# A rotary embedding on one core: a cast store of zeros at the head of the software queue, and batch 0 stored in one piece

## The chip, the core and the metric

The kernel runs on one core of a Trainium2 chip. The core has several engines that run side by side, each on its own instruction stream: VectorE (DVE in the profile) does elementwise arithmetic, ScalarE (ACT) copies and casts here, GpSimd (POOL) issues most of the transfers, SyncE (SP) issues a few others. The transfers themselves are done by 16 DMA engines, which are fed by two queues: a software queue (q0 in the profile, "software_dynamic"), whose transfers POOL issues, and a hardware queue (q1, "hardware_dynamic"), whose transfers SP issues. The transfers of the software queue can change the number type on the way (here float32 in memory, float16 on chip); this is called a cast load or a cast store below.

The metric is the device time of one execution in microseconds (us). Lower is better.

## The reference

`x` has 8 batches of 2048 positions, 16 heads and 64 elements a head, all float32; `cos` and `sin` have 2048 positions of 32 elements.

```python
x1 = x[..., :head_dim // 2]
x2 = x[..., head_dim // 2:]
cos = cos[None, :, None, :]
sin = sin[None, :, None, :]
out1 = x1 * cos - x2 * sin
out2 = x1 * sin + x2 * cos
return np.concatenate([out1, out2], axis=-1)
```

So 8 MiB of float32 are read and 8 MiB are written for each of the 8 batches, and each element meets two multiplications and one addition.

## The kernel before

**Layout.** A batch is one tile `xt` of 128 partitions. Each partition holds 16 consecutive positions (rows, `J = 16`), of 1024 elements each. On the chip the data is float16. There are five buffers for `xt` (`NBUF = 5`), so a load into a buffer has to wait until the store of the batch that used it five batches earlier has landed: the load of batch 5 waits for the store of batch 0, that of batch 6 for the store of batch 1, that of batch 7 for the store of batch 2.

**Loads.** Batch 0 comes in two parts. Its first two rows (`JA = 2`) come through the hardware queue as float32 into `head` (L36, the first transfer that SP issues), and ACT casts them into the tile (L84). SP then issues the loads of `sin_f` (L44) and `cos_f` (L45). The other 14 rows of batch 0 and all rows of the other batches are cast loads of the software queue, issued by POOL in `load` (L52).

**Arithmetic.** `rotate` does three VectorE instructions over rows `j0` to `j1` of a batch: `v = swapped halves * sin` (L73), `xt = xt * cos` (L79), `xt = xt + v` (L81). `sin_h` has a negative sign in its first half (ACT, L88 and L89), `cos_h` is a cast copy (ACT, L90). Batch 0 is rotated in two calls, first the 2 rows of `head`, then the other 14.

**Stores.** `store` (L60) issues one cast store for a batch on the software queue. Batch 0 is the exception: its row 0 (of 16) goes out alone as `first` (L100), 512 KB, and its rows 1 to 15 follow as a store of 7680 KB. The last batch leaves in three parts: rows 0 to 8 (L130, called `gate`), rows 9 to 13 (L132), and the last two rows, which ACT casts to float32 (L140) and SP stores through the hardware queue (L141), once `gate` has landed.

**Order.** The software queue works through its transfers in the order in which POOL issues them. A planner in the framework orders the instructions of each engine by the program's order and by when it thinks that each can start; the kernel adds a few edges by hand (`add_manual_dep` with `NoSync`, which order the two instructions on their engine and add no wait on a transfer). By hand, `first` stands behind the load of batch 3, the load of batch 4 behind `first`, and the rest of batch 0 behind `first`. In the profile POOL's order is: loads 0, 1, 2, 3; `first`; load 4; the rest of store 0; store 1; loads 5 and 6; stores 2 and 3; load 7; stores 4, 5 and 6; the two parts of batch 7.

Of the kernel before, what the change touches and what calls it, by code (L numbers as in the profile page):

```python
# [1 line left out]

# [4 lines left out]


@with_exitstack  # L10
def kernel(
    ctx: ExitStack,
    tc: tile.TileContext,
    x: bass.AP,
    cos: bass.AP,
    sin: bass.AP,
    out: bass.AP,
):
    nc = tc.nc
    f16 = mybir.dt.float16  # L20
    f32 = mybir.dt.float32

    B, S, H, D = x.shape
    Dh = D // 2
    P = nc.NUM_PARTITIONS
    J = S // P
    NBUF = 5

    const_pool = ctx.enter_context(tc.tile_pool(name="rope_const", bufs=1))
    io_pool = ctx.enter_context(tc.tile_pool(name="rope_io", bufs=NBUF))  # L30
    tmp_pool = ctx.enter_context(tc.tile_pool(name="rope_tmp", bufs=1))

    JA = 2
    head = const_pool.tile([P, JA, H, D], f32)
    x0 = x[0].rearrange("(p j) h d -> p j (h d)", j=J)
    nc.sync.dma_start(  # L36
        out=head.rearrange("p j h d -> p (j h d)"),
        in_=x0[:, 0:JA, :].rearrange("p j f -> p (j f)"),
    )
    sin_f = const_pool.tile([P, J, Dh], f32)  # L40
    cos_f = const_pool.tile([P, J, Dh], f32)
    cos_h = const_pool.tile([P, J, Dh], f16)
    sin_h = const_pool.tile([P, J, D], f16)
    nc.sync.dma_start(out=sin_f, in_=sin.rearrange("(p j) d -> p j d", j=J))  # L44
    nc.sync.dma_start(out=cos_f, in_=cos.rearrange("(p j) d -> p j d", j=J))  # L45

    loads = []

    def load(b):
        xt = io_pool.tile([P, J, H, D], f16)  # L50
        j0 = JA if b == 0 else 0
        dma = nc.gpsimd.dma_start(  # L52
            out=xt[:, j0:J, :, :].rearrange("p j h d -> p (j h d)"),
            in_=x[b].rearrange("(p j) h d -> p j (h d)", j=J)[:, j0:J, :].rearrange("p j f -> p (j f)"),
        )
        loads.append(dma)
        return xt

    def store(b, xt, j0=0):
        return nc.gpsimd.dma_start(  # L60
            out=out[b].rearrange("(p j) h d -> p j (h d)", j=J)[:, j0:J, :].rearrange("p j f -> p (j f)"),
            in_=xt[:, j0:J, :, :].rearrange("p j h d -> p (j h d)"),
        )

    def rotate(xt, j0, j1):
        v = tmp_pool.tile([P, J, H, D], f16)
        n = j1 - j0
        js = slice(j0, j1)
        shape = [P, n, H, 2, Dh]
        sin_b = sin_h[:, js, :].rearrange("p j (e d) -> p j e d", e=2).unsqueeze(2).to_broadcast(shape)  # L70
        cos_b = cos_h[:, js, :].unsqueeze(2).to_broadcast([P, n, 2 * H, Dh])
        xe = xt[:, js, :, :].rearrange("p j h (e d) -> p j h e d", e=2)
        nc.vector.tensor_mul(  # L73
            out=v[:, js, :, :].rearrange("p j h (e d) -> p j h e d", e=2),
            in0=xe[:, :, :, ::-1, :],
            in1=sin_b,
        )
        xw = xt[:, js, :, :].rearrange("p j h (e d) -> p j (h e) d", d=Dh)
        nc.vector.tensor_mul(out=xw, in0=xw, in1=cos_b)  # L79
        xa = xt[:, js, :, :].rearrange("p j h d -> p (j h d)")  # L80
        nc.vector.tensor_add(out=xa, in0=xa, in1=v[:, js, :, :].rearrange("p j h d -> p (j h d)"))  # L81

    tiles = [load(b) for b in range(NBUF - 1)]
    nc.scalar.copy(  # L84
        out=tiles[0][:, 0:JA, :, :].rearrange("p j h d -> p (j h d)"),
        in_=head.rearrange("p j h d -> p (j h d)"),
    )
    nc.scalar.copy(out=sin_h[:, :, Dh:D], in_=sin_f)  # L88
    nc.scalar.mul(out=sin_h[:, :, 0:Dh], in_=sin_f, mul=-1.0)  # L89
    nc.scalar.copy(out=cos_h, in_=cos_f)  # L90
    rotate(tiles[0], 0, JA)
    def part(b, j0, j1):
        return (
            out[b].rearrange("(p j) h d -> p j (h d)", j=J)[:, j0:j1, :].rearrange("p j f -> p (j f)"),
            tiles[b][:, j0:j1, :, :].rearrange("p j h d -> p (j h d)"),
        )

    def store_rows(b, j0, j1):
        dst, src = part(b, j0, j1)
        return nc.gpsimd.dma_start(out=dst, in_=src)  # L100

    first = store_rows(0, 0, 1)
    tc.add_manual_dep(
        first.ins,
        loads[NBUF - 2].ins.name,
        mybir.DependencyInfo(mybir.DependencyClass.NoSync, mybir.DependencyReason.DATA),
        reason="order of the ring",
    )
    tiles.append(load(NBUF - 1))
    tc.add_manual_dep(  # L110
        loads[NBUF - 1].ins,
        first.ins.name,
        mybir.DependencyInfo(mybir.DependencyClass.NoSync, mybir.DependencyReason.DATA),
        reason="order of the ring",
    )
    for b in range(B):
        rotate(tiles[b], JA if b == 0 else 0, J)
        if b < B - 1:
            st = store(b, tiles[b], 1 if b == 0 else 0)
            if b == 0:  # L120
                tc.add_manual_dep(
                    st.ins,
                    first.ins.name,
                    mybir.DependencyInfo(mybir.DependencyClass.NoSync, mybir.DependencyReason.DATA),
                    reason="order of the ring",
                )
        if b + NBUF < B:
            tiles.append(load(b + NBUF))
    dst, src = part(B - 1, 0, 9)
    gate = nc.gpsimd.dma_start(out=dst, in_=src)  # L130
    dst, src = part(B - 1, 9, J - JA)
    rest = nc.gpsimd.dma_start(out=dst, in_=src)  # L132
    tc.add_manual_dep(
        rest.ins,
        gate.ins.name,
        mybir.DependencyInfo(mybir.DependencyClass.NoSync, mybir.DependencyReason.DATA),
        reason="order of the ring",
    )
    dst, src = part(B - 1, J - JA, J)
    nc.scalar.copy(out=head.rearrange("p j h d -> p (j h d)"), in_=src)  # L140
    end = nc.sync.dma_start(out=dst, in_=head.rearrange("p j h d -> p (j h d)"))  # L141
    tc.add_manual_dep(
        end.ins,
        gate.ins.name,
        mybir.DependencyInfo(mybir.DependencyClass.Sync, mybir.DependencyReason.DATA),
        reason="the last rows go out behind this part",
    )


# [1 line left out]
_INS = ['x', 'cos', 'sin']  # L151
_OUTS = [((8, 2048, 16, 64), 'float32')]


# [23 lines left out]
```

## Time and profile before

| | |
|---|---|
| Time, median of 3 runs | 317.0 us (316.9 to 317.13) |
| Profiled execution, its own time | 317.48 us |
| Profiled execution, its span | 315.7 us |
| VectorE busy | 209.1 us (66%) |
| ScalarE busy | 6.8 us (2%) |
| GpSimd busy | 9.9 us (3%) |
| Software queue | 2592 packets, 99.09 MB, 98.1% of 16 engines |
| Hardware queue | 576 packets, 2.62 MB, 2.3% of 16 engines |
| Memory read and written | 67.63 MB and 67.11 MB, 427 GB/s over the span |

The span is what the trace covers; the run's own time lies 1.8 us above it. The megabytes of a queue are counted at the destination, so a cast load counts half of what it reads from memory. A share over 100% in a short window is a matter of counting: a packet is booked wholly where it starts. "Landing" is the moment at which a transfer's completion is signalled; a row that gives "us to landing" counts from the issue.

### The profile page before, as it was taken

Reading aid. Unit: us, or ns where it says so; the run is one execution under the profiler, and the core shown is the slowest. Engines: PE = TensorE matmul, PEld = TensorE weight load, DVE = VectorE, ACT = ScalarE, POOL = GpSimd, SP = SyncE. Lnnn points to the kernel's source line nnn. Section 1 sums busy time; section 2 is a strip of 40 time slices with the busy share of each in tenths; the row PEclk is TensorE's granted clock in tenths of the full one; section 3 lists DMA queues with packets and bytes.
Section 4 is the critical chain, followed back from the end, with each engine's and each line's share of the span. In section 5 each row is a group of like instructions: output and inputs, shape, how many; then the busy total and the mean of one; then the engine's idle time right before and its main releaser. Section 6 shows DMA issues by size and latency. Waiting matters only on the chain.

```text
span 315.7 us, 122 instructions
## 1 busy us (share of the span) xinstructions
DVE 209.1 (66%) x27; ACT 6.8 (2%) x6; POOL 9.9 (3%) x22
## 2 busy tenths in 40 slices
DVE  0010699999999999999999999994009994000000
ACT  4100000000000000000000000000000002000000
POOL 3000100000000000001000000100000001000000
DMA  9899999999999989999999999999999999999998
GB/s 277 183 262 208 199 220 245 199 199 199 266 199 199 498 374 523 399 332 241 224 199 199 390 407 399 399 531 266 199 249 482 399 399 515 415 399 399 432 434 330
DMA packets 3168, 101.71 MB, mean 322 GB/s; under 512 B 352, under 2 KB 352, under 8 KB 736
## 3 DMA queue, kind: packets, MB, share of 16 engines
q0 software_dynamic: 2592, 99.09, 98.1%
q1 hardware_dynamic: 576, 2.62, 2.3%
HBM read 67.63 MB, written 67.11 MB: 427 GB/s over the span
## 4 chain that ended last, share of the span: by engine, by line
DVE 25%; DMA 22%; issue 18%; another core or an unknown queue 17%; POOL 1%; ACT 1%; SPq 0%; POOLq 0%; DVEq 0%; ACTq 0%
DMA xt<-in_x_dram 12%; DMA cos_f<-in_cos_dram 10%; DVE xt L79 8%; DVE xt L81 8%; DVE v L73 8%; ACT head L140 1%; POOL out_dram L60 1%; POOL xt L52 0%; ACT cos_h L90 0%; SPq L44 0%; SPq L36 0%; POOLq L52 0%; POOLq L60 0%; DVEq L73 0%
## 5 line engine op out<-in xcount | busy, mean ns | idle before, releaser
L73 DVE TENSOR_TENSOR v<-xt,sin_h 128x16384 f16<-128x16384 f16 (+2 forms) x9 | 69.7, 7744 | 36.8 <-DMA xt<-in_x_dram 20.7
L79 DVE TENSOR_TENSOR xt<-xt,cos_h 128x16384 f16<-128x16384 f16 (+2 forms) x9 | 69.7, 7744 | 17.5 <-ACT cos_h L90 17.2
L81 DVE TENSOR_TENSOR xt<-xt,v 128x16384 f16<-128x16384 f16 (+2 forms) x9 | 69.7, 7744 | 0.3
L52 POOL DMA_DIRECT2D xt<-in_x_dram x8 | 4.4, 557 | 111.1 <-DMA out_dram<-xt 110.3
L140 ACT CAST head<-xt 128x2048 f32<-128x2048 f16 x1 | 1.9, 1897 | 229.5 <-DVE xt L81 229.5
L60 POOL DMA_DIRECT2D out_dram<-xt x7 | 3.7, 535 | 63.9 <-DVE xt L81 63.9
L130 POOL DMA_DIRECT2D out_dram<-xt x1 | 0.5, 531 | 46.3 <-DVE xt L81 46.3
L84 ACT CAST xt<-head 128x2048 f16<-128x2048 f32 x1 | 1.9, 1897 | 3.6 <-DMA head<-in_x_dram 3.6
L100 POOL DMA_DIRECT2D out_dram<-xt x1 | 0.5, 541 | 33.5 <-DVE xt L81 33.5
L84 ACT ACT_TABLE_LOAD x1 | 1.3, 1283 | 0.7 <-PEq L162 0.7
L90 ACT CAST cos_h<-cos_f 128x512 f16<-128x512 f32 x1 | 0.6, 618 | 17.8 <-DMA cos_f<-in_cos_dram 17.8
L88 ACT CAST sin_h<-sin_f 128x512 f16<-128x512 f32 x1 | 0.6, 617 | 7.2 <-DMA sin_f<-in_sin_dram 7.2
L89 ACT ACTIVATE sin_h<-sin_f 128x512 f16<-128x512 f32 x1 | 0.6, 624 | 0.0
L132 POOL DMA_DIRECT2D out_dram<-xt x1 | 0.5, 531 | 0.0
L162 POOL MEMSET const-float32-0.0<- 128x1 f32 x1 | 0.1, 99 | 0.2 <-issue 0.2
L162 POOL MEMSET const-bfloat16-1.0<- 128x1 bf16 x1 | 0.1, 102 | 0.0
L162 POOL MEMSET const-float32-1.0<- 128x1 f32 x1 | 0.1, 99 | 0.0
L162 POOL MEMSET const-uint8-127<- 128x1 uint8 x1 | 0.1, 99 | 0.0
## 6 DMA issues: line engine op xcount, KB each, us to landing
xt<-in_x_dram POOLq DMA_DIRECT2D x7, 4096.0 KB, 41.3
out_dram<-xt POOLq DMA_DIRECT2D x1, 7680.0 KB, 61.6
out_dram<-xt POOLq DMA_DIRECT2D x1, 4608.0 KB, 42.4
xt<-in_x_dram POOLq DMA_DIRECT2D x1, 3584.0 KB, 22.3
out_dram<-xt POOLq DMA_DIRECT2D x1, 2560.0 KB, 47.9
head<-in_x_dram SPq DMA_DIRECT2D x1, 1024.0 KB, 4.8
out_dram<-head SPq DMA_DIRECT2D x1, 1024.0 KB, 8.4
out_dram<-xt POOLq DMA_DIRECT2D x1, 512.0 KB, 47.1
```

The costliest lines, as they stand in the source:

```text
L52: dma = nc.gpsimd.dma_start(out=xt[:, j0:J, :, :].rearrange("p j h d -> p (j h d)"), in_=x[b].rearrange("(p j) h d -> p j (h d)", j=J)[:, ...
L60: return nc.gpsimd.dma_start(out=out[b].rearrange("(p j) h d -> p j (h d)", j=J)[:, j0:J, :].rearrange("p j f -> p (j f)"), in_=xt[:, j0:J ...
L73: nc.vector.tensor_mul(out=v[:, js, :, :].rearrange("p j h (e d) -> p j h e d", e=2), in0=xe[:, :, :, ::-1, :], in1=sin_b,)
L79: nc.vector.tensor_mul(out=xw, in0=xw, in1=cos_b)
L81: nc.vector.tensor_add(out=xa, in0=xa, in1=v[:, js, :, :].rearrange("p j h d -> p (j h d)"))
L84: nc.scalar.copy(out=tiles[0][:, 0:JA, :, :].rearrange("p j h d -> p (j h d)"), in_=head.rearrange("p j h d -> p (j h d)"),)
L88: nc.scalar.copy(out=sin_h[:, :, Dh:D], in_=sin_f)
L89: nc.scalar.mul(out=sin_h[:, :, 0:Dh], in_=sin_f, mul=-1.0)
L90: nc.scalar.copy(out=cos_h, in_=cos_f)
L100: return nc.gpsimd.dma_start(out=dst, in_=src)
L130: gate = nc.gpsimd.dma_start(out=dst, in_=src)
L140: nc.scalar.copy(out=head.rearrange("p j h d -> p (j h d)"), in_=src)
```

## The change

1. A small tile `z` of 128 partitions by 256 float16 elements is set to zero by POOL.
2. POOL issues a cast store of `z` to the first 256 elements of each partition's part of `out[0]`: 1 KB of float32 a partition, 128 KB in all. The store of batch 0 writes the result over these places later.
3. All five loads, batches 0 to 4, follow; an edge by hand puts the load of batch 0 behind the opening store.
4. `store_rows` and `first` are gone, and with them the edges around them. Batch 0 is stored whole, 8192 KB, by the same call as the other batches.

```diff
-    tiles = [load(b) for b in range(NBUF - 1)]
+    z = const_pool.tile([P, 256], f16)
+    nc.gpsimd.memset(z, 0.0)
+    opening = nc.gpsimd.dma_start(
+        out=out[0].rearrange("(p j) h d -> p j (h d)", j=J)[:, 0:256],
+        in_=z,
+    )
+    tiles = [load(b) for b in range(NBUF)]
+    tc.add_manual_dep(
+        loads[0].ins,
+        opening.ins.name,
+        mybir.DependencyInfo(mybir.DependencyClass.NoSync, mybir.DependencyReason.DATA),
+        reason="order of the ring",
+    )
...
-    def store_rows(b, j0, j1):
-        dst, src = part(b, j0, j1)
-        return nc.gpsimd.dma_start(out=dst, in_=src)
-
-    first = store_rows(0, 0, 1)
-    tc.add_manual_dep(
-        first.ins,
-        loads[NBUF - 2].ins.name,
...
-    tiles.append(load(NBUF - 1))
-    tc.add_manual_dep(
-        loads[NBUF - 1].ins,
-        first.ins.name,
...
     for b in range(B):
         rotate(tiles[b], JA if b == 0 else 0, J)
         if b < B - 1:
-            st = store(b, tiles[b], 1 if b == 0 else 0)
-            if b == 0:
-                tc.add_manual_dep(
-                    st.ins,
-                    first.ins.name,
...
+            store(b, tiles[b])
         if b + NBUF < B:
             tiles.append(load(b + NBUF))
```

More of the change, by code (lines that the diff above doesn't have):

```diff
@@ L81, in rotate @@
         nc.vector.tensor_add(out=xa, in0=xa, in1=v[:, js, :, :].rearrange("p j h d -> p (j h d)"))
-    tiles = [load(b) for b in range(NBUF - 1)]
+    z = const_pool.tile([P, 256], f16)
+    nc.gpsimd.memset(z, 0.0)
+    opening = nc.gpsimd.dma_start(
+        out=out[0].rearrange("(p j) h d -> p (j h d)", j=J)[:, 0:256],
+        in_=z,
[7 more added lines that the diff above has]
+    )
     nc.scalar.copy(
@@ L96, in part @@
         )
-    def store_rows(b, j0, j1):
-        dst, src = part(b, j0, j1)
-        return nc.gpsimd.dma_start(out=dst, in_=src)
-    first = store_rows(0, 0, 1)
-    tc.add_manual_dep(
-        first.ins,
-        loads[NBUF - 2].ins.name,
-        mybir.DependencyInfo(mybir.DependencyClass.NoSync, mybir.DependencyReason.DATA),
-        reason="order of the ring",
-    )
-    tiles.append(load(NBUF - 1))
-    tc.add_manual_dep(
-        loads[NBUF - 1].ins,
-        first.ins.name,
-        mybir.DependencyInfo(mybir.DependencyClass.NoSync, mybir.DependencyReason.DATA),
-        reason="order of the ring",
-    )
     for b in range(B):
@@ L118 @@
         if b < B - 1:
-            st = store(b, tiles[b], 1 if b == 0 else 0)
-            if b == 0:
-                tc.add_manual_dep(
-                    st.ins,
-                    first.ins.name,
-                    mybir.DependencyInfo(mybir.DependencyClass.NoSync, mybir.DependencyReason.DATA),
-                    reason="order of the ring",
-                )
+            store(b, tiles[b])
         if b + NBUF < B:
```

## The prediction

> **What bounds the kernel now.** I read the page's queue totals first, then the chain of waits, then the issues of each transfer with their time to landing, and last short windows of the DMA view.
>
> ```profile
> DVE 209.1 (66%) x27; ACT 6.8 (2%) x6; POOL 9.9 (3%) x22
> q0 software_dynamic: 2592, 99.09, 98.1%
> q1 hardware_dynamic: 576, 2.62, 2.3%
> HBM read 67.63 MB, written 67.11 MB: 427 GB/s over the span
> POOL xt L52 <- DMA out_dram<-xt: 110.3, 3, 56.0
> DVE v L73 <- DMA xt<-in_x_dram: 20.7, 1, 20.7
> ```
>
> The 16 DMA engines are full (98.1% plus 2.3%); no other engine is above 66%. VectorE still waits 20.7 us for the last load. So the time is the work of the DMA engines from their first packet to their last, plus any gap. The gap at the front and the hold-up of `cos_f` are seen in these rows (timeline; then the DMA view of 0 to 5.27 us, and of 5.27 to 34 us):
>
> ```profile
> 1.25 2.26 POOL L52 DMA_DIRECT2D xt<-in_x_dram  x4 [0.81 <-PEq L173]
> 33.63 0.62 ACT L90 CAST cos_h<-cos_f 128x512 f16<-128x512 f32 x1 [17.81 <-DMA cos_f<-in_cos_dram]
> ...
> q1 hardware_dynamic: 209, 1.18, 65.6%
> ...
> q0 software_dynamic: 224, 6.29, 101.7%
> q1 hardware_dynamic: 223, 0.39, 4.0%
> ```
>
> Up to 5.27 us there are hardware packets only: the first load, issued at 1.25, sends its first packet 4.0 us later. From then on the queues alternate packet by packet, and the short packets of `sin_f` and `cos_f` wait behind long load packets; that is why `cos_f` lands at 33.6.
>
> Landings follow from issue plus time to landing (issue rows): load 0 1.25+22.3 = 23.6; load 1 1.92+41.3 = 43.2; load 2 2.44+60.3 = 62.7; load 3 2.96+79.9 = 82.9; `first` 37.06+47.1 = 84.2; load 4 37.59+65.9 = 103.5; rest of store 0 60.04+61.6 = 121.6; load 5 122.19+38.0 = 160.2; load 6 141.62+37.9 = 179.5. The differences are what each costs on the queue: load 2 19.5, load 3 20.1, `first` 1.3, load 4 19.3, load 6 19.3. Loads ahead of the first store are slower than those behind it. The DMA view shows where; these are the software rows of windows 52.1 to 52.6, 71.7 to 72.2, 79.1 to 79.6 and, behind the first store, 92.9 to 93.5:
>
> ```profile
> q0 software_dynamic: 16, 0.52, 519.1%
> ...
> q0 software_dynamic: 16, 0.52, 515.5%
> ...
> q0 software_dynamic: 16, 0.52, 594.3%
> ...
> q0 software_dynamic: 16, 0.52, 405.3%
> ```
>
> Each window holds one packet start per engine. Share times width is the mean packet: 2.60, 2.58, 2.97 and 2.43 us. So all 16 engines together lost 0.17, 0.15 and 0.54 us, 0.85 in all, at three places before the first store; I found none behind it in 230 us, among them four whole loads.
>
> **The change part by part.**
>
> *Memset and one more issue on POOL.* POOL's constant memsets take 0.10 us; 256 elements I bound by 0.1 to 0.4. One issue takes 0.53 to 0.67 (L52 rows). With a short wait of the opening on the memset, load 0 is issued about 1.0 us later and, if its 4.0 us stay, sends its first packet at 6.3 instead of 5.28. Its cover is hardware work: behind 5.27 the hardware queue still has 4.0% of 28.7 us = 1.15 us per engine when interleaved, some 1.0 back to back, and the opening store itself adds 0.4. That reaches to 6.7. Cost nothing; without the cover 1.0 us. Loads 1 to 4 are queued behind on POOL and shift alike, unseen, since the queue reaches load 1 only at 23 us. SP issues in the old order.
>
> *The opening store.* No row shows 1 KB pieces. `first` has 128 pieces of 4 KB and cost 1.33 us; by bytes a quarter is 0.33 (lower end). From above: eight packets per engine at the 0.08 to 0.096 us of the 2 KB hardware packets are 0.64 to 0.77. The nearest is `first`: eight packets in 1.33 us are 0.166 each, against 0.151 for its share (1/16 of 19.3, over 8), so 0.015 is per packet; 1 KB is 0.038+0.015 = 0.053, eight are 0.42. I take +0.4.
> By the Trainium skill, "DMA: Bandwidth & Descriptors", section on the anatomy of a DMA on the gpsimd path, a transfer has a fixed 2.0 us and the rest by bytes, so this one would be 2.3 us and the forecast 1.9 us higher, which speaks against the change; `first` by that rule would be 3.2 us and took 1.33 between landings, so here the fixed part lies beside other transfers.
>
> *`first` goes, store 0 whole.* 1.33 becomes 19.3/16 = 1.21: -0.12 (0 to -0.12). Store 0 is issued when VectorE has finished batch 0, at 60 or earlier; the queue reaches it at about 102, so that wait is hidden by 40 us. `load 4` loses its wait for `first`; it was never late.
>
> *`sin_f` and `cos_f` drain early.* In the extra microsecond they go out back to back: 1.15 becomes about 1.0, so -0.2 to 0; I take -0.15. `cos_f` lands near 7 instead of 33.6, and VectorE starts batch 0 at load 0's landing (about 24) instead of 36.8. That gains nothing by itself: it will then wait for load 2, load 3, load 5 and load 7.
>
> *The slow packets.* All before a store had gone through the queue, none after. If that order is the cause, the opening store removes 0.85 us (by the landings against 19.3, 0.2+0.8 = 1.0). If the cause is another, 0; if loads queued ahead of a real store suffer, load 4 now does too, and at load 3's price that is +0.8. I take -0.85: three losses in 80 us, then none in 230, is hard to get by accident.
>
> *Buffers.* Load 5 still waits for store 0 (landing at 121.6 less about 0.7), with store 1 queued to cover it, 19 us long; loads 6 and 7 likewise (covers: load 5, store 3). The queue never runs dry.
>
> Sum, against the profiled run's own 317.48: +0.4 -0.12 -0.15 -0.85 = -0.72, so 316.76. The median lies 0.48 below the profiled run: 316.28. I say 316.3. A change under 0.2% (0.63 us) can't be told from none here.
>
> **The rivals.**
>
> *The slow packets have another cause* (time since the start, neighbours, VectorE). For it: one starts at 52.16, 0.04 us after VectorE's L81; the others have no such partner. Against it: nothing like it in the later loads. Then +0.4 -0.12 -0.15 = +0.13: 317.1, no change that can be told.
>
> *The software queue starts late: slower.* If the 4.0 us between issue and first packet are paid by each transfer in turn, the opening sends at about 5.8 and load 0 4.0 later, at 9.8. Cover ends at 6.7: 3.1 us of idle engines, at the front, given to nobody: 316.3+3.1 = 319.4. It ends slower from a first load packet later than 6.7+0.7+0.63 = about 8.0. For it: only one such start is in the trace, and POOL spent 2.26 us on four issues inside it. Against: load 1's packets follow load 0's without a gap, so descriptions are made ahead when several are queued.
>
> *The planner orders POOL otherwise.* If load 5 came ahead of store 1 on POOL, it would wait for store 0's landing with the queue empty and store 1 behind it: 0.58 us from landing to issue (121.61 to 122.19) and up to 4.0 to the first packet, 4.6 us for each such load, 321 with one. For it: the edges behind `first` go, and loads 6 and 7 already wait where the cover is one transfer. Against: store 0 and load 5 stand to each other as before. A milder form costs nothing: if load 1 slips ahead of the opening, load 0 lands at about 43, and VectorE starts 6.4 us later than before, against 20.7 us of its waiting at load 7.
>
> **How the numbers follow.** Forecast case 0.50 (faster by over 0.2% in 0.45, the rest same), another cause 0.23 (same 0.18, slower 0.05), late start 0.14 (slower 0.12, same 0.02), other order 0.13 (slower). Faster 0.45, same 0.25, slower 0.30. Low: 317.0 +0.33 -0.12 -0.2 -1.0 = 316.0, less 0.2 for the scatter of the three runs: 315.8. High: the case of another cause with the opening at 0.77 and no savings, 317.8, and part of the late start: 318.2. The forecast case alone: 315.8 to 316.8.
>
> **What would show it.** Right: software packets of short size before 6.5 us and no idle engine between 5 and 7; `cos_h` cast near 7; loads 1 to 4 landing 19.3 apart with no packet over 2.5 us; load 0's first packet by 6.7; POOL's order opening, loads 0 to 4, stores 0 and 1, loads 5 and 6. Wrong: a hole in the DMA share before 10 us; load 2 and load 3 still at 19.5 and 20.1; POOL waiting for a store's landing with nothing queued.

## The result and the profile after

The changed kernel takes 317.6 us in the median of 20 runs (317.13 to 318.06), the kernel before 317.0 (316.73 to 317.36). The ratio is 1.002, interval [1.0014, 1.0026]: slower by 0.6 us. The time lies inside the range on record (315.8 to 318.2), on the other side of no change from the forecast of 316.3. (In the kernel the opening's target is `out[0].rearrange("(p j) h d -> p (j h d)", j=J)[:, 0:256]`, all elements of a partition in one dimension; the diff ahead of the prediction has `p j (h d)` there.)

The totals of the changed kernel, and last POOL's waits for stores (total, times, longest):

```profile
DVE 209.1 (66%) x27; ACT 6.7 (2%) x6; POOL 10.2 (3%) x23
q0 software_dynamic: 2592, 99.22, 98.1%
q1 hardware_dynamic: 576, 2.62, 2.3%
HBM read 67.63 MB, written 67.24 MB: 427 GB/s over the span
POOL xt L52 <- DMA out_dram<-xt: 119.4, 3, 56.0
```

Nothing has changed in kind: the DMA engines are full, and 0.13 MB more are written. The start, from the timeline of the changed kernel (start, duration, instruction, and in brackets the idle time ahead of it):

```profile
0.73 0.31 POOL L84 MEMSET z<- 128x256 f16 x1 [0.29 <-POOLq L149]
1.35 0.67 POOL L85 DMA_DIRECT2D out_dram<-z  x1 [0.31 <-POOL z L84]
2.02 2.66 POOL L52 DMA_DIRECT2D xt<-in_x_dram  x5
7.51 0.61 ACT L100 CAST sin_h<-sin_f 128x512 f16<-128x512 f32 x1
24.35 0.62 ACT L102 CAST cos_h<-cos_f 128x512 f16<-128x512 f32 x1 [15.70 <-DMA cos_f<-in_cos_dram]
```

The opening is issued at 1.35 and load 0 at 2.02, 0.77 later than before; load 0's first packet starts at 5.92 instead of 5.28. In the DMA view of the changed kernel, hardware packets alone run up to 5.4 us; the next row is of 5.4 to 6.5 us, in which both queues are at work:

```profile
q1 hardware_dynamic: 232, 1.23, 65.9%
...
q0 software_dynamic: 128, 0.26, 104.2%
q1 hardware_dynamic: 140, 0.25, 78.9%
```

There is no hole ahead of load 0's packets: while the opening is sent, packets of the hardware queue go out as well (`sin_f` lands at 6.7). POOL's order is as forecast: opening, loads 0 to 4, stores 0 and 1, loads 5 and 6.

And the row on which the forecast stood. In the changed kernel's DMA view of 98.2 to 98.9 us, the last packets of load 4:

```profile
q0 software_dynamic: 16, 0.52, 438.2%
```

Share times width, over the 16 engines' one packet each, is 3.07 us a packet, against 2.43 without disturbance: 0.63 us lost by all 16 engines. It is the only such place in this execution. The slow packets of loads 2 and 3 are not there, but new ones stand at the end of load 4. Both first profiles were also off their medians: 317.48 where the kernel before has 317.0, 317.35 where the changed one has 317.6. So the first experiments looked at both kernels again and took the change apart.

### The profile page after: what moved, and what is told of

Same layout as the page of the kernel before. It is cut to its first block, busy times and chain, and to the rows that moved or that the text cites. A ratio compares the mean times of both kernels' runs of the same rounds, so it can differ in the third digit from the quotient of the medians.

```text
span 315.6 us, 125 instructions
## 1 busy us (share of the span) xinstructions
DVE 209.1 (66%) x27; ACT 6.7 (2%) x6; POOL 10.2 (3%) x23
## 3 DMA queue, kind: packets, MB, share of 16 engines
q0 software_dynamic: 2592, 99.22, 98.1%
## 4 chain that ended last, share of the span: by engine, by line
DVE 25%; another core or an unknown queue 20%; DMA 19%; issue 18%; POOL 1%; ACT 1%; SPq 0%; POOLq 0%; DVEq 0%; ACTq 0%
DMA xt<-in_x_dram 12%; DVE xt L81 8%; DVE xt L79 8%; DVE v L73 8%; DMA cos_f<-in_cos_dram 7%; ACT head L127 1%; POOL out_dram L60 0%; POOL xt L52 0%; ACT cos_h L102 0%; SPq L44 0%; SPq L36 0%; POOLq L60 0%; DVEq L73 0%; ACTq L127 0%
## 5 line engine op out<-in xcount | busy, mean ns | idle before, releaser
L85 POOL DMA_DIRECT2D out_dram<-z x1 | 0.7, 665 | 0.3 <-POOL z L84 0.3
```

The source lines that it names most:

```text
L85: opening = nc.gpsimd.dma_start(out=out[0].rearrange("(p j) h d -> p (j h d)", j=J)[:, 0:256], in_=z,)
```

## The experiments

"Slow packets" below is the time lost by the 16 engines in the last packets of one load, from windows like the last one. Medians are given beside the kernel before in the same session (316.84 to 317.0).

In the diffs `behind(a, b)` stands for an edge by hand that puts `a` behind `b` in POOL's order and adds no wait.

**1. The two kernels again, and each half of the change alone.**

`opening_alone` is the kernel before with this put in front of its loads:

```diff
+    z = const_pool.tile([P, 256], f16)
+    nc.gpsimd.memset(z, 0.0)
+    opening = nc.gpsimd.dma_start(
+        out=out[0].rearrange("(p j) h d -> p (j h d)", j=J)[:, 0:256],
+        in_=z,
+    )
     tiles = [load(b) for b in range(NBUF - 1)]
+    behind(loads[0], opening)
```

> The kernel before with the opening store put in front; `first` and the split of store 0 stay. Theory A (the price is the opening's: its packets and a later start of the loads; the slow packets are chance): the whole loss is here, 317.0 + 0.6 + 0.12 = about 317.7. Theory B (the price is the loss of `first`: five loads then run ahead of the first real store, and slow packets come with such loads): the opening costs next to nothing by itself, 317.1, at most 317.2. Theory C (the forecast: an early store removes slow packets, something else took it back): 316.5 or less, with no packet of loads 1 to 3 over 2.5 us.

`whole_alone` is the changed kernel without the opening:

```diff
-    z = const_pool.tile([P, 256], f16)
-    nc.gpsimd.memset(z, 0.0)
-    opening = nc.gpsimd.dma_start(
...
     tiles = [load(b) for b in range(NBUF)]
-    behind(loads[0], opening)
```

> Five loads, then store 0 in one piece; no `first`, no opening store. Theory A: `first` was 0.12 us dearer than its share, so 316.9. Theory B: 317.5 to 317.7, with slow packets of 0.8 to 0.9 us in sum ahead of store 0. Theory C: load 4 now runs ahead of any store too, 317.2 to 317.8, slow packets in loads 1 to 4; it differs from B only in that opening_alone is then below 317.0.

`before_again` and `after_again` have no edit.

> The kernel before once more, for a second profile. The first profiled execution was 0.48 us above the median and had 0.85 us of slow packets. Theory A and any theory in which slow packets are chance: the sum of the slow packets is another here, and the execution's time moves with it (0.4 us of slow packets at a time of 317.0). Theory C: 0.85 us again, at 52, 72 and 79 us.

> The changed kernel once more, for a second profile. Its first profiled execution, 317.35, was 0.25 us below its median of 317.6 and had 0.64 us of slow packets, all in the last packets of load 4. If the slow packets make the scatter, an execution at 317.6 has some 0.9 us of them. If the median's loss is a gap at the front, the first packet of load 0 is later than the 5.92 us of the first profile in step with the time.

Measured against 316.84: opening alone 317.22, ratio 1.0009 [1.0, 1.0018]; whole alone 317.39, 1.0014 [1.0005, 1.0023]; before again 316.96, 0.9999 [0.999, 1.0008]; after again 317.58, 1.0019 [1.001, 1.0028]. Both halves cost something, though the interval of the opening touches no change. B comes nearest: it had the cost of whole alone, but allowed the opening 0.2 us at most. A has whole alone wrong, and C falls, since the early small store brought no gain.

The second profile of the kernel before (its execution took 316.97 us) has slow packets in one place only, the end of load 3. Window 78.4 to 79.2:

```profile
q0 software_dynamic: 16, 0.52, 359.4%
```

That is 2.88 us a packet, 0.44 lost. The 0.16 and 0.15 us at 52 and 72 us are gone, and no profile of any other kernel has them: they belonged to one execution. `opening_alone` loses 0.32 at the end of load 3; `whole_alone`, and `after_again` (window 98.1 to 98.9), lose more, and at the end of load 4. The first row is `whole_alone`, window 97.9 to 98.4, the second `after_again`:

```profile
q0 software_dynamic: 16, 0.52, 679.7%
```

```profile
q0 software_dynamic: 16, 0.52, 423.4%
```

These are 3.40 and 3.39 us a packet, 0.97 and 0.96 lost. So the loss at the end of the last load ahead of the first real store comes in every one of these six profiles, the opening of 128 KB does not take it away, and it is larger where five loads run first.

The chain of waits gives the size of the whole change. These are its rows for load 7 (issue, time to landing), in `before_again`, the changed kernel, `after_again` and `whole_alone`:

```profile
198.69 38.25 DMA xt<-in_x_dram
```

```profile
199.03 38.33 DMA xt<-in_x_dram
```

```profile
199.52 38.31 DMA xt<-in_x_dram
```

```profile
199.19 38.27 DMA xt<-in_x_dram
```

In the first three load 7 lands at 236.94, 237.36 and 237.83 us, 0.42 and 0.89 later than before, 0.65 in the mean. The opening's part is seen at load 2, ahead of any slow packets. These are its rows (DMA view of the stretch of its issue: size, time to landing) in `before_again`, issued at 2.43, and in the changed kernel, issued at 3.08:

```profile
xt<-in_x_dram POOLq DMA_DIRECT2D x1, 4096.0 KB, 60.0
```

```profile
xt<-in_x_dram POOLq DMA_DIRECT2D x1, 4096.0 KB, 59.8
```

To the hundredth it lands at 62.48 without the opening and, in the two executions, at 62.91 and 62.88 with it: 0.4 behind. With the slow packets taken off (0.44, 0.63 and 0.96), load 7 lands at 236.50, 236.73 and 236.87, so 0.2 and 0.4 of this are left there. The end of `first` does not explain the rest: `whole_alone`, which has no `first` either, lands load 7 at 237.46, 0.52 later than `before_again`, and its slow packets alone are 0.53 more. Between the two executions of the changed kernel the slow packets differ by 0.33 of the 0.47 us. Load 0's first packet differs too (5.92 and 6.05), but at load 2 the two are level.

**2. Where must a store stand, and what is it behind?** The zero store of 1 KB a partition is moved between the loads (m is 0, 2 or 3), with five loads and store 0 whole:

```diff
-    tiles = [load(b) for b in range(NBUF)]
+    tiles = [load(b) for b in range(m + 1)]
...
+    zs = zeros(0)
+    behind(zs, loads[m])
+    for b in range(m + 1, NBUF):
+        tiles.append(load(b))
+        behind(loads[b], zs)
```

> No opening store, no `first`; the 1 KB zero store stands between load 0 and load 1, then loads 1 to 4 and store 0 whole. Every profile so far loses 0.3 to 1.0 us in the last packets of the last load ahead of the first real store (load 3 at 80 us where `first` follows, load 4 at 98 us where store 0 follows) and nothing at later changes from load to store. D1 (the first change from loads to any store is dear): the slow packets stand at the end of load 0, about 22 us, none ahead of store 0. D2 (the price grows with the loads in a row): none at load 0, 0.4 to 0.5 us at the end of load 4 (four in a row, as before), time 317.3. D3 (only the change to the first large store is dear): 0.6 to 1.0 us at the end of load 4, time 317.7. D4 (the price is at the end of what was issued at the start): as D3.

> The same with the zero store between load 2 and load 3. D1: slow packets at the end of load 2, 62 us, none at the end of load 4; 317.2 to 317.5. D2: at most 0.3 us at the end of load 2 (three in a row), nothing at the end of load 4 (two in a row, as later in the kernel); 316.9 to 317.1. D3 and D4: 0.6 to 1.0 us at the end of load 4; 317.7.

> The same with the zero store between load 3 and load 4: at the place of `first`, with a quarter of its bytes, and load 4 issued at the start. D1 and D2: 0.3 to 0.55 us at the end of load 3, none at the end of load 4; 317.1 to 317.3. D3 and D4: nothing at load 3, 0.6 to 1.0 us at the end of load 4; 317.7.

In the last of this group load 4 waits for the first rotation, with no zero store:

```diff
-    tiles = [load(b) for b in range(NBUF)]
+    tiles = [load(b) for b in range(NBUF - 1)]
...
-    rotate(tiles[0], 0, JA)
+    turned = rotate(tiles[0], 0, JA)
+    tiles.append(load(NBUF - 1))
+    tc.add_manual_dep(
+        loads[NBUF - 1].ins,
+        turned.ins.name,
+        mybir.DependencyInfo(mybir.DependencyClass.Sync, mybir.DependencyReason.DATA),
...
```

> Five loads, store 0 whole, no zero store; load 4 is issued only when the first two rows of batch 0 are rotated, at 37 us as in the kernel before. D4: slow packets at the end of load 3, 80 us. D1, D2, D3: as in whole_alone, 0.6 to 1.0 us at the end of load 4, 317.4.

Measured against 316.91: 317.48, 317.45, 317.41 and 317.51. All four lose time at the end of load 4, at 98 us: 0.71, 0.69, 0.68 and 0.83 us. At the zero store itself no more than 0.04 us is lost. In the second kernel, windows 59.1 to 59.9 (end of load 2, ahead of the zeros) and 98.2 to 98.9 (end of load 4):

```profile
q0 software_dynamic: 16, 0.52, 304.0%
...
q0 software_dynamic: 16, 0.52, 446.2%
```

2.43 us a packet, then 3.12. D1, D2 and D4 fall; D3 stands, though the times lie 0.2 to 0.3 below its 317.7: small stores do not count. In a running queue the 128 KB store of the second kernel took 0.42 us between landings (62.56 to 62.98), which is the 0.42 that the prediction worked out from `first`.

**3. The size or the place of the first real store.** `first` (row 0, 512 KB) is put behind load 4, or behind load 1, or behind load 1 with row 1 behind load 3; or it is cut to 128 KB of real results in its old place. The core of each edit:

`first_behind_load4`:

```diff
+    tiles = [load(b) for b in range(NBUF)]
...
+    behind(first, loads[NBUF - 1])
```

`first_behind_load1`, and below the line of dots what `rows_behind_loads_1_and_3` has on top:

```diff
+    behind(first, loads[1])
+    behind(loads[2], first)
...
+    second = store_rows(0, 1, 2)
+    behind(second, loads[3])
+    behind(loads[4], second)
```

`quarter_first`, where `flat_out` and `flat_in` are batch 0 with all of a partition's elements in one dimension:

```diff
-    first = store_rows(0, 0, 1)
+    first = nc.gpsimd.dma_start(out=flat_out[:, 0:256], in_=flat_in[:, 0:256])
```

> The kernel before with load 4 issued at the start and `first` (row 0, 512 KB) behind load 4 instead of load 3. Without slow packets the kernels with `first` come to a span of 314.75 us, a time of 316.5. L (the price grows with the time that loads have run with no large store between them; a 128 KB store does not count): five loads, 0.6 to 1.0 us at the end of load 4, time 317.1 to 317.5. S (the first large store pays once, less where it is cut in 4 KB pieces): 0.3 to 0.55 us at the end of load 4, time 316.8 to 317.1.

> `first` behind load 1 (its rows are ready at 37 us, load 1 ends at 43), loads 2 to 4 behind it, then the rest of store 0. L: nothing at the end of load 1 (two loads in a row, as later in the kernel where no slow packets are), up to 0.3 us at the end of load 4 (three in a row); time 316.5 to 316.8. S: 0.3 to 0.55 us at the end of load 1, at 41 us, and nothing at load 4; time 316.8 to 317.1, like the kernel before.

> Row 0 behind load 1, row 1 behind load 3, rows 2 to 15 behind load 4: no more than two loads in a row anywhere. One more small store costs 0.12 us. L: no slow packets at all; time 316.6, 0.3 under the kernel before. S: 0.3 to 0.55 us at the end of load 1; time 317.0.

> The kernel before with `first` cut to a quarter of row 0 (1 KB of float32 a partition, real results from the tile), the rest of batch 0 in one store behind load 4. If the size decides (L or S): slow packets at the end of load 4, 0.6 to 1.0 us, none at load 3, time 317.2 to 317.5, as with 1 KB of zeros in the same place. If it decides that the bytes come from the tile and not from the small tile of zeros: 0.3 to 0.55 us at the end of load 3, none at load 4, time 316.9.

Measured against 316.92: 317.33 (0.88 us lost at the end of load 4), 316.88 (0.32 at the end of load 1, none later), 316.86 (0.36 at the end of load 1, none later) and 317.02 (0.56 at the end of load 4). The end of load 1 in the second kernel, window 39.8 to 40.4:

```profile
q0 software_dynamic: 16, 0.52, 459.4%
```

2.76 us a packet. Neither theory is whole. S is right that the price is paid once and by the first large store, L that it is larger behind five loads than behind two or four. That the bytes are real results does not matter: `quarter_first` has its slow packets where the zeros of the same size had them. Its time, 317.02, lies below the 317.2 to 317.5 expected. Moving `first` forward brings no gain that can be told: ratios 1.0 [0.9992, 1.0009] and 0.9998 [0.9989, 1.0006].

**4. A large opening, and an early `first`.** `opening_512KB` makes the changed kernel's opening four times as large; `xt0` is batch 0's tile:

```diff
-    z = const_pool.tile([P, 256], f16)
-    nc.gpsimd.memset(z, 0.0)
+    nc.vector.memset(xt0[:, 0:1, :, :].rearrange("p j h d -> p (j h d)"), 0.0)
     opening = nc.gpsimd.dma_start(
-        out=out[0].rearrange("(p j) h d -> p (j h d)", j=J)[:, 0:256],
-        in_=z,
+        out=out[0].rearrange("(p j) h d -> p (j h d)", j=J)[:, 0:1024],
+        in_=xt0[:, 0:1, :, :].rearrange("p j h d -> p (j h d)"),
...
+        behind(loads[b], loads[b - 1])
```

> The changed kernel with an opening store four times as large: 4 KB of float32 a partition, 512 KB, taken from row 0 of batch 0's tile (zeroed first; the result of ACT's cast comes into it when the opening has landed). So far the slow packets come once, in the load ahead of the first store of 512 KB or more: 0.32 to 0.37 us behind two loads, 0.3 to 0.54 behind four, 0.56 to 1.0 behind five, whatever small stores went before. P1 (the first large store pays, wherever it stands): with this opening no slow packets at the end of load 4; span 314.70 + 1.33 - 0.15 + up to 0.35 = 315.9 to 316.2, time 317.6 to 318.0. P2 (it pays for the loads ahead of it, so an opening of any size is for nothing): 0.64 to 1.0 us at the end of load 4, time 318.3 to 318.7.

`first_behind_load0` lets SP load `sin_f` and `cos_f` ahead of `head` and puts `first` behind load 0:

```diff
-    nc.sync.dma_start(
-        out=head.rearrange("p j h d -> p (j h d)"),
...
     nc.sync.dma_start(out=sin_f, in_=sin.rearrange("(p j) d -> p j d", j=J))
     nc.sync.dma_start(out=cos_f, in_=cos.rearrange("(p j) d -> p j d", j=J))
+    nc.sync.dma_start(
+        out=head.rearrange("p j h d -> p (j h d)"),
...
+    behind(first, loads[0])
+    behind(loads[1], first)
```

> The kernel before with SP's order turned round (`sin_f`, `cos_f`, then `head`), so that the first two rows are rotated by about 20 us, and `first` behind load 0, loads 1 to 4 behind it. P1 and a price that falls with the loads ahead: 0.1 to 0.3 us of slow packets at the end of load 0, none at load 4; span 314.75 - 0.1 + 0.2 = 314.85, time 316.6, 0.3 below the kernel before. If the price does not fall below 0.32: time 316.75. If load 1, issued behind `first` at about 19 us, comes too late for the queue, which ends load 0 at 23.6: a gap of up to 1 us there and no gain.

The large opening takes the slow packets away. `opening_512KB`, window 99.3 to 100.2, the end of load 4:

```profile
q0 software_dynamic: 16, 0.52, 270.2%
```

2.43 us a packet, nothing lost there, as P1 said. Yet the kernel takes 318.14 us, over P1's 317.6 to 318.0, ratio 1.0037 [1.0023, 1.005]. Its span, which has no slow packets, is 316.37, that of `whole_alone` without them 315.72 - 0.97 = 314.75: the large opening costs 1.62 us. It cures 0.55 to 0.97.

`first_behind_load0` failed for another reason. Its first two rows came late (timeline):

```profile
26.03 1.90 ACT L93 CAST xt<-head 128x2048 f16<-128x2048 f32 x1 [20.74 <-DMA head<-in_x_dram]
32.02 0.53 POOL L109 DMA_DIRECT2D out_dram<-xt  x1 [30.11 <-DVE xt L81]
```

Behind `sin_f` and `cos_f`, the packets of `head` alternated with load 0's and landed at 26.0 instead of 5.6; the queue ran dry (DMA share 0.01 from 25 to 30 us). 327.55 us, ratio 1.0323 [1.0302, 1.0344]. It tells little of the price, and what it tells does not fit: 0.90 us were lost at the end of load 4 although `first` had gone before. The sixteen first packets of load 1, right behind `first`, were slow as well: 2.97 us in the mean, from 34.4 us on.

**5. Bytes or pieces, and one load ahead.** Against `opening_512KB`, in the order of the expectations: the opening cut into pieces (`out=`, and the source alike), cut to 32 partitions, and moved behind load 0:

```diff
-        out=out[0].rearrange("(p j) h d -> p (j h d)", j=J)[:, 0:1024],
+        out=out[0].rearrange("(p j) h d -> p j (h d)", j=J)[:, 0:4, 0:256],
...
-        out=out[0].rearrange("(p j) h d -> p (j h d)", j=J)[:, 0:1024],
+        out=out[0].rearrange("(p j) h d -> p (j h d)", j=J)[0:32, 0:1024],
...
-    behind(loads[0], opening)
+    behind(opening, loads[0])
+    behind(loads[1], opening)
```

> As opening_512KB, which had no slow packets and took 318.14 us, but its 4 KB a partition go to four places of 1 KB (rows 0 to 3). If the bytes of a store decide whether it counts: no slow packets again, 318.1 and up to 0.4 us more for four times as many pieces. If the size of its pieces decides (1 KB pieces never counted so far): slow packets of 0.64 to 1.0 us at the end of load 4, 318.8 to 319.2.

> As opening_512KB, but 32 of the 128 partitions only: 128 KB in 4 KB pieces. If the bytes decide: slow packets of 0.56 to 1.0 us at the end of load 4; time 318.14 - 1.0 (three quarters of 1.33) + 0.6 to 1.0 = 317.7 to 318.1. If the size of the pieces decides: none, 317.1 to 317.2.

> The 512 KB of zeros between load 0 and load 1, in a running queue. first_behind_load0 ran the queue dry for 9.5 us ahead of `first`, and its slow packets came at the end of load 4 (0.9 us) although `first` had gone before. Q1 (a large store counts where it follows loads without a gap): here 0.1 to 0.35 us at the end of load 0, none at the end of load 4; span 314.70 + 1.33 + 0.1 to 0.35 = 316.1 to 316.4, time 317.9 to 318.1. Q2 (a large store counts only until some 60 us have passed, which the gap and four loads exceeded): slow packets at the end of load 4 here too, 77 us behind the store; time 318.4 to 318.8.

Measured against 317.0: 318.2 with no slow packets; 317.55 with 0.55 us at the end of load 4; 318.01 with 0.38 us at the end of load 0 and none at load 4. The third kernel, windows 20.4 to 21.3 (packets of load 0 take 2.13 us undisturbed) and 99.4 to 100.1:

```profile
q0 software_dynamic: 16, 0.46, 278.7%
...
q0 software_dynamic: 16, 0.52, 347.4%
```

2.51 us a packet, then 2.43. Of the openings, the one of 512 KB ends the slow packets in pieces of 1 KB as in pieces of 4 KB, the one of 128 KB in neither: the bytes decide, not the pieces. Q1 holds, with 0.38 us a little over its 0.1 to 0.35. Behind load 0 the 512 KB cost less than at the front: 316.20 - 0.38 - 314.75 = 1.07 us.

All profiles together, the time lost ahead of the first store of 512 KB or more, by the loads that ran before it:

| Loads ahead | Slow packets, us |
|---|---|
| 0 (openings of 512 KB) | none seen |
| 1 | 0.38 |
| 2 | 0.32, 0.36 |
| 4 | 0.32, 0.44, 0.54 |
| 5 | 0.55, 0.56, 0.63, 0.68, 0.69, 0.71, 0.83, 0.88, 0.96, 0.97 |

`first_behind_load0` is not in the table: its queue had run empty ahead of `first`.

The scatter of the times does not follow the price. The three kernels that lose nothing, or 0.38 us at load 0, stay within 0.11 to 0.17 us over five runs (318.04 to 318.2; 318.1 to 318.27; 317.97 to 318.08), those with five loads ahead within 0.4 to 0.9 over eight to twenty; but with two loads ahead it is 0.60 and 0.43 over eleven.

## Why the prediction was wrong

- *What bounds the kernel* was right: the sum of DMA work is the time, and of 0.4 us added at the front 0.2 to 0.4 are still there at load 7.
- *The opening store, +0.4*: right. 0.42 between landings in a running queue, 0.4 at the landing of load 2. The fixed 2 us that the Trainium skill ("DMA: Bandwidth & Descriptors", section "Anatomy of one DMA — SWDGE (gpsimd) path") would add did not show.
- *One more issue on POOL, nothing*: right. Load 0 was issued 0.77 us later, and hardware packets and the opening filled the time. The rival of a late start fell (load 0's first packet came at 5.92, not at 9.8), and so did that of another order on POOL.
- *`first` goes, -0.12*: not seen. `whole_alone` against `before_again` leaves 0.01 us at load 7 once the slow packets are taken off.
- *`sin_f` and `cos_f` drain early, -0.15*: `sin_f` landed at 6.7 instead of 14.7, `cos_f` at 24.3 instead of 33.6, not near 7. No gain is seen at the landing of load 2, which is later by the opening's whole 0.4.
- *The slow packets, -0.85*: this step failed, and with it the sign. Its argument was "All before a store had gone through the queue, none after", and it took that an opening of 128 KB is such a store. Only stores of 512 KB or more ended the slow packets, 128 KB never did, in seven kernels. And the end of `first`, a 512 KB store behind four loads, left store 0 behind five loads as the first large one. The step had named that end of its range: "if loads queued ahead of a real store suffer, load 4 now does too". In place of -0.85 stand +0.2 to +0.5 (0.63 and 0.96 against 0.44). The rival of another cause, with 317.1, was nearer to 317.6, but it put the price of a fifth load at nothing.
- The size was misread too. 0.31 of the 0.85 us came in no other execution, and the page had a sign of it: the profiled run lay 0.48 above the median. Of the two places at 52 and 72 us I had made evidence for a rule. And the sum took these 0.31 us off twice: within the 0.85, and again with the 0.48 from the profiled run down to the median.

Sum as measured at load 7: +0.2 to +0.4 for the opening, nothing for `first`, +0.2 to +0.5 for slow packets, 0.4 to 0.9 in all; the medians say 0.6. That the time lies inside the range is no support for the forecast: the forecast case alone reached from 315.8 to 316.8, and the part above it belonged to the rivals.

## What to carry to other kernels

When the profiled run lies off the median by as much as the effect that is to be explained, take a second profile before building on the first: here a third of the effect was one execution's. Where the DMA engines are full from end to end, each transfer that is added costs time (here 0.42 us for 128 KB in a running queue, 1.07 and 1.62 for 512 KB), so a preparation has to save more than it moves. Before a large store is replaced by a small one that "does the same", find out whether its size is what works.

## What the runs showed of the hardware

In 16 of the 19 profiles the first store of 512 KB or more is preceded by one slow last packet on all 16 engines: 0.3 to 0.4 us behind one or two loads, 0.3 to 0.5 behind four, 0.55 to 0.97 behind five. In these, later changes from loads to stores cost nothing, and only the first profile of the kernel before has slow packets elsewhere. In two profiles that store is an opening with no load ahead of it, and no slow packet was seen at all. A 128 KB store does not end the slow packets, in pieces of 1 or 4 KB; between loads, with zeros or results in pieces of 1 KB, it does not bring them about either. A 512 KB store in pieces of 4 KB does both; in pieces of 1 KB it was tried as an opening only, and ended them.

What it is, no run shows. Where between 128 and 512 KB the limit lies, and whether loads or time set the price, was not tried. One profile contradicts the rule: `first_behind_load0` lost 0.90 us at the end of load 4 with a 512 KB store before it, one that had met an empty queue; whether that matters is open.
